# TensorE's instructions from the memory attention to the third head's state put into the program's own order, with dense matmuls dealt out behind each small step

## The chip, the cores and the metric

One core of one Trainium2 chip. The metric is device time in microseconds (us) of one launch. The kernel before was timed three times: median 1388.3 us, from 1385.67 to 1389.44.

## The reference, cut to what matters

One layer of a hybrid decoder, 1024 tokens of width 1024, all in fp32. One input projection feeds four HGRN2 heads (a gated recurrence), a sparse attention whose indexer picks 256 keys per query, and an attention into 256 memory tokens. Their outputs go through one output projection, and a SwiGLU feed-forward follows.

```python
h = rmsnorm(x, norm_mix[layer])
hq, hf, hi, hg, sq, sk, sv, iq, ik, iw, mq = split_in(h @ w_in[layer])
o_hg = hgrn2_mix(...)      # 4 heads; per chunk: o = q exp(b) S + (decayed q k^T) v; S = exp(b_last) S + k^T v
o_sa = dsa_mix(...)        # score, _, idx = lax.top_k(score, topk); softmax over the kept keys
o_mem = mem_mix(...)       # softmax(q k^T) v over 256 memory tokens
mixed = jnp.concatenate([o_hg, o_sa, o_mem], axis=-1)
x = x + (mixed @ w_out[layer]).astype(x.dtype)
a, b = jnp.split(rmsnorm(x, norm_ffn[layer]) @ w_ffn_in[layer], 2, axis=-1)
x = x + ((jax.nn.silu(a) * b) @ w_ffn_out[layer]).astype(x.dtype)
```

## The kernel before, in words

Every fp32 operand of a large product is split into a high and a low part, and the product is made of three passes (high by high, high by low, low by high). A projection of 128 output channels (`proj`, L165-190) is 24 matmuls of 128x512 for each half of the tokens, 48 in all; they are the dense work of the middle of the kernel. A page of weights comes by DMA through a staging tile (`load_page`, L117-L118): ScalarE (ACT) writes the high part, GpSimd (POOL) or VectorE (DVE) the low part. PSUM is used as four pairs of banks: `mm` for projections, `lg`, `sm` and `rc` for small products.

The stretch that the change touches goes from about 149 us (the indexer's scores are done) to 561 us (the sparse attention's softmax begins). It holds, in the order of the program's text:

- `hgrn_v(0)`: values of heads 0 and 1, token-major (`token_major`, L457: 192 matmuls of 128x256 into two `lg` and two `sm` banks, then eight scaled copies on ACT, L466).
- `memory_attention` (L689-724): 16 units, for 8 blocks of 128 tokens by 2 pairs of heads. A unit is logits (L697), maximum on DVE (L701), two Exp on ACT (L704), reciprocal (L706), scaling on POOL (L708), four transposes (L713), a copy (L715 on ACT or L717 on DVE), values (L722), a copy out (L724).
- for each head `hgrn_proj` (three projections of 48 matmuls, taken out of PSUM on DVE, L485), `hgrn_gates` (ACT and POOL), `hgrn_intra` (eight levels: a small product, L518 or L553, then `descend`: Q on DVE L527, K on POOL L528, F on DVE L529, and a masked copy L543), `hgrn_state` (transposes L571, L578, output products L594/L596, the square sums and norm on DVE L602/L144-151/L606, transposes L612, L613).
- sparse values (`token_major(4)`), sparse queries (pages 20 and 21), sparse keys (`sparse_keys`, pages 18 and 19, normed on DVE: L739, L144-151, L169, L172, L744), later split into the stacked keys `kst` (L811) and queries `qst` (L254).
- `bisect`, the top-k: 31 rounds over the bits of a threshold; a round counts scores, on DVE for blocks 7 and 4 (L646), on ACT as Sign for blocks 6, 5, 3 and 2 (L643), with a few tiny DVE operations (L638, L648, L655, L658) between the rounds.

No engine runs in the text's order. The kernel is built under a scheduler that simulates the engines (L1362: `schedule_with_timeline_sim=True`) and lays down one instruction list per engine; on the chip each engine runs its list strictly in order. So dense matmuls stand between small steps where the scheduler put them, and the bisection's counts fill DVE and ACT beside them.

All weight pages are issued from SP's queue. What the names in the rows are: `mat_` memory attention, `hg_` HGRN2, `sap_` projections and norms of the sparse attention, `sat_` the sparse attention itself, `idx_` indexer and top-k; `_mm`, `_lg`, `_sm`, `_rc` are the PSUM pairs, `whi`/`wlo` weights, `xn_h` the normed input.

Of the kernel before, what the change touches and what calls it, by code (L numbers as in the profile page):

```python
# [42 lines left out]
def hybrid_block(ctx, tc, xT, memT, wch, wikw, wv, wkm, wvm, woa, wob, wfi, wfo,  # L43
                 vec, cst, lvl, out):
    nc = tc.nc
    V, S, G, T = nc.vector, nc.scalar, nc.gpsimd, nc.tensor
# [400 lines left out]
    def token_major(g0):  # L447

        acc = [bank("lg"), bank("lg"), bank("sm"), bank("sm")]
        for g in range(2):  # L450
            w = load_page(wv[g0 + g], 4, 256)
            for tt in range(8):
                o = acc[tt // 2][:, 256 * (tt % 2):256 * (tt % 2) + 256]
                i = 0
                for pw, p in PASSES:
                    for k in range(4):
                        T.matmul(o, H[p][4 * g + k][tt // 4][:, bs(tt % 4)], w(pw, k),  # L457
                                 start=g == 0 and i == 0 and tt % 2 == 0,
                                 stop=g == 1 and i == 11 and tt % 2 == 1)
                        i += 1  # L460
        return [a.rearrange("p (t d) -> p t d", t=2) for a in acc]

    def scaled_rows(dst, acc):

        for tt in range(8):
            S.activation(dst[tt // 4][:, tt % 4, :], acc[tt // 2][:, tt % 2, :], AF.Copy,  # L466
                         scale=rn[:, tt:tt + 1])

    def hgrn_v(pair):
        ph[0] = "hg"  # L470
        Vp = [xt(10 + j, [128, 4, 256]) if pair else mt(4 + j, (128, 4, 256)) for j in range(2)]
        scaled_rows(Vp, token_major(2 * pair))
        for j in range(2):
            Vh[2 * pair + j] = lambda c, j=j: Vp[c // 4][:, c % 4, bs(j)]

    def hgrn_proj(h):
        ph[0] = "hg"
# [5 lines left out]
        for i, t in enumerate((Q, F, Gt)):  # L483
            proj(page(6 + 3 * h + i), 128, H,
                 lambda ps, hf: V.tensor_mul(t[:, hs(hf)], ps, rrow[:, hs(hf)]))  # L485
# [202 lines left out]
    def memory_attention():  # L688
        ph[0] = "mat"  # L689
        Pm, PTm = mt(2, (128, 2, 2, 256)), mt(3, (128, 2, 2, 2, 128))  # L690
        for b in range(8):
            for m in range(2):
                P, PT = Pm[:, m], PTm[:, m]
                lg = bank("lg").rearrange("p (j k) -> p j k", j=2)
                for j in range(2):
                    for p in range(2):
                        T.matmul(lg[:, j, :], mqs[2 * m + j][:, b // 4, bs(b % 4)],  # L697
                                 kms[m][:, j, p, :], start=p == 0, stop=p == 1)
                mx = np_.tile([128, 2], F32, tag="mx", name=nm("mx"))
                sm = np_.tile([128, 2], F32, tag="sm", name=nm("sm"))  # L700
                V.tensor_reduce(mx, lg, axis=AX.X, op=ALU.max)  # L701
                V.scalar_tensor_tensor(mx, mx, -1.0, qrs[:, m, b, :], op0=ALU.mult, op1=ALU.mult)
                for j in range(2):
                    S.activation(P[:, j, :], lg[:, j, :], AF.Exp, bias=mx[:, j:j + 1],  # L704
                                 scale=qrs[:, m, b, j:j + 1], accum_out=sm[:, j:j + 1])
                V.reciprocal(sm, sm)  # L706
                for j in range(2):
                    G.tensor_scalar(P[:, j, :], P[:, j, :], sm[:, j:j + 1], 1.0, op0=ALU.mult,  # L708
                                    op1=ALU.mult)
                tb = bank("rc").rearrange("p (j k q) -> p j k q", j=2, k=2)  # L710
                for j in range(2):
# [12 lines left out]
                S.activation(M[6 + m][:, bs(b)], po[:, 0:128], AF.Copy)  # L724
# [3 lines left out]
    def sparse_keys():  # L728
        ph[0] = "sap"
        kr.extend((mt(4), mt(5)))  # L730
        for m in range(2):
            def evac_k(ps, hf, m=m):
# [3 lines left out]
                S.activation(sq, ps, AF.Square)  # L736
                ss = bank("sm")
# [16 lines left out]
    def sparse_queries():  # L754
# [3 lines left out]
        def evac_q0(ps, hf):  # L758
            sums_q(qsq[:, 0], ps, hf)
            S.activation(sqr[0][:, hs(hf)], ps, AF.Copy)  # L760
# [605 lines left out]
```

## Time and profile before

| what | value |
|---|---|
| median of three runs | 1388.3 us |
| lowest, highest run | 1385.67, 1389.44 us |
| the profiled execution | 1389.85 us |
| its span | 1388.1 us |
| mean granted TensorE clock | 0.969 |
| busy share of the span, PE / DVE / ACT / POOL | 94% / 77% / 50% / 34% |

The span is the profiled time from the first instruction to the last; 1.75 us of the execution lie outside it. Busy shares are averages over stages with different limits: the busy time by stretch says more. Matmul durations overlap, so the cost of one matmul is read from the distance between starts.

### The profile page before, as it was taken

The numbers are of one execution on the slowest core, as the hardware profiler recorded it, in microseconds if no ns is written. First come the engines' busy times: TensorE is split into PE (matmuls) and PEld (weight loads), VectorE is DVE, ScalarE is ACT, GpSimd is POOL, SyncE is SP. The second block draws the span as 40 slices with busy tenths as digits, with TensorE's granted clock in tenths as the row PEclk, the third lists the DMA queues.
The fourth block names the chain that finished last, engine by engine and source line by source line (L and its number), as shares of the span: only waits on it lengthen the run. The fifth ranks groups of instructions, "written<-read, shape, count | busy, mean of one in ns | idle before, by whom it ended". The sixth has DMA issues, their size and how long they took to land.

```text
span 1388.1 us, 22034 instructions
## 1 busy us (share of the span) xinstructions
PE 1304.1 (94%) x8072; PEld 1067.2 (77%) x8072; DVE 1062.2 (77%) x2094; ACT 692.6 (50%) x1369; POOL 473.9 (34%) x395
## 2 busy tenths in 40 slices
PE   6989999988989995999997999999999998999998
PEld 4767787768878884776886888888888886878887
DVE  8697998896469689775579777777787766696764
ACT  7555879856853243657354333333333333334442
POOL 2311033355257632424005233332332310474520
PEclk9999999989999995899999999999999999999999
DMA  6210010000010001013331332223223219654241
GB/s 236 68 39 16 32 47 16 32 32 32 31 48 31 26 26 47 2 61 112 129 117 61 114 108 106 91 91 107 99 103 105 89 59 354 233 192 142 84 145 61
DMA packets 53244, 122.19 MB, mean 88 GB/s; under 512 B 6032, under 2 KB 6160, under 8 KB 53136
## 3 DMA queue, kind: packets, MB, share of 16 engines
q1 hardware_dynamic: 52848, 120.58, 25.4%
q8 instruction: 63, 1.03, 0.3%
q14 instruction: 45, 0.37, 0.1%
q10 hardware_dynamic: 288, 0.22, 0.1%
HBM read 92.19 MB, written 28.57 MB: 87 GB/s over the span
## 4 chain that ended last, share of the span: by engine, by line
PE 59%; DVE 6%; ACT 2%; issue 1%; POOL 1%; DMA 1%; ACTq 0%; DVEq 0%; POOLq 0%
PE ff_lg L1095 17%; PE ff_rc L1095 12%; PE fo_mm L1258 4%; PE fo_sm L1258 4%; PE wo_mm L1054 3%; PE fo_rc L1258 3%; PE fo_lg L1258 3%; PE wo_sm L1054 2%; PE sap_mm L186 2%; PE hg_mm L186 2%; PE sat_sm L856 1%; PE sat_lg L830 1%; PE wo_mm L186 1%; PE sat_rc L875 1%; PE sat_mm L875 1%
## 5 line engine op out<-in xcount | busy, mean ns | idle before, releaser
L117 ACT ACTIVATE ff_whi<-ff_x 128x512 fp32r<-128x512 f32 x112 | 70.0, 629 | 125.1 <-PE ff_rc L1095 69.1
L643 ACT ACTIVATE idx_x<-idx_x,packs 128x896 int8<-128x896 f32 (+3 forms) x128 | 105.7, 826 | 42.9 <-DVE packs L638 37.0
L1095 PE MATMUL ff_lg<-wo_h,ff_whi 128*128 128x512 f32 x396 | 104.3, 390 | 0.0
L186 PE MATMUL hg_mm<-xn_h,hg_whi 128*128 128x512 f32 x384 | 97.0, 396 | 0.0
L1095 PE MATMUL ff_rc<-wo_h,ff_whi 128*128 128x512 f32 x308 | 90.8, 395 | 0.0
L1095 PE MATMUL ff_lg<-wo_x,ff_whi 128*128 128x512 f32 x308 | 83.8, 400 | 5.3 <-ACT ff_tmp L1102 4.8
L118 DVE TENSOR_TENSOR ff_wlo<-ff_x,ff_whi 128x512 fp32r<-128x512 f32 x112 | 82.6, 746 | 6.9 <-ACT ff_whi L117 4.0
L1095 PEld LDWEIGHTS ff_lg<-wo_h,ff_whi 128*128 128x128 f32 x396 | 74.5, 188 | 15.5
L186 PEld LDWEIGHTS hg_mm<-xn_h,hg_whi 128*128 128x128 f32 x384 | 70.7, 188 | 14.5 <-issue 0.7
L118 POOL TENSOR_TENSOR hg_wlo<-hg_wst,hg_whi 128x512 fp32r<-128x512 f32 x32 | 42.9, 1353 | 104.9 <-ACT hg_whi L117 79.8
L1095 PEld LDWEIGHTS ff_lg<-wo_x,ff_whi 128*128 128x128 f32 x308 | 56.8, 189 | 23.8 <-ACT ff_whi L117 7.4
L646 DVE TENSOR_SCALAR_CACHE_REDUCE idx_x<-idx_x,packs 128x1024 int8<-128x1024 f32 x64 | 68.8, 1074 | 0.9
L1095 PEld LDWEIGHTS ff_rc<-wo_h,ff_whi 128*128 128x128 f32 x308 | 58.8, 191 | 12.5
L1095 PE MATMUL ff_rc<-wo_x,ff_whi 128*128 128x512 f32 x220 | 64.4, 390 | 0.1
L528 POOL TENSOR_TENSOR hg_x<-hg_x,hg_x 128x256 f32<-128x256 f32 x56 | 48.5, 881 | 30.4 <-PE hg_rc L518 18.8
L1095 PE MATMUL ff_lg<-wo_h,ff_wlo 128*128 128x512 f32 x198 | 55.6, 389 | 0.0
L388 DVE SCALAR_TENSOR_TENSOR idx_x<-idx_tmp,packs,idx_x 128x512 f32<-128x512 f32 (+2 forms) x70 | 46.1, 712 | 10.6 <-ACT idx_tmp L383 10.3
L118 DVE TENSOR_TENSOR fo_wlo<-fo_tmp,fo_whi 128x512 fp32r<-128x512 f32 x33 | 33.2, 1007 | 27.0 <-ACT fo_whi L117 27.0
L186 PE MATMUL hg_mm<-xn_h,hg_wlo 128*128 128x512 f32 x192 | 50.8, 397 | 0.0
L1095 PEld LDWEIGHTS ff_rc<-wo_x,ff_whi 128*128 128x128 f32 x220 | 41.2, 188 | 9.1 <-ACT ff_whi L117 0.6
L118 DVE TENSOR_TENSOR fo_wlo<-fo_h,fo_whi 128x512 fp32r<-128x512 f32 x31 | 32.0, 1033 | 19.0 <-ACT fo_whi L117 19.0
L1095 PE MATMUL ff_rc<-wo_h,ff_wlo 128*128 128x512 f32 x154 | 45.6, 389 | 0.0
(484 smaller groups left out, 3679.0 us busy)
## 6 DMA issues: line engine op xcount, KB each, us to landing
gd<-ff_m SPq DMA_DIRECT2D x77, 256.0 KB, 2.0
fo_x<-gd SPq DMA_DIRECT2D x77, 256.0 KB, 4.0
ff_x<-wfi SPq DMA_DIRECT2D x16, 512.0 KB, 3.3
ff_wst<-wfi SPq DMA_DIRECT2D x14, 512.0 KB, 3.3
ff_m<-wfi SPq DMA_DIRECT2D x14, 512.0 KB, 3.3
hg_wst<-wch SPq DMA_DIRECT2D x12, 512.0 KB, 3.3
fo_x<-wfo SPq DMA_DIRECT2D x24, 256.0 KB, 5.2
fo_h<-wfo SPq DMA_DIRECT2D x20, 256.0 KB, 4.2
```

Source lines behind the costliest of these rows:

```text
L117: S.activation(hi, src, AF.Copy)
L118: (eng or V).tensor_sub(lo, src, hi.bitcast(F32))
L186: T.matmul(ps[:M, :], w(pw, k), h[p][k][hf], start=i == 0, stop=i == len(order) - 1)
L388: V.scalar_tensor_tensor(sc[b][:, c0:c1], rl[:, :c1 - c0], iww[:, b, h:h + 1], sc[b][:, c0:c1], op0=ALU.mult, op1=ALU.add)
L528: G.tensor_mul(Kv[:, :, 0, :], Kv[:, :, 0, :], fr.to_broadcast([128, n, w]))
L643: S.activation(waste[S][:, :nk], sc[b], AF.Sign, bias=nf[:, j:j + 1], accum_out=ct[:, j:j + 1])
L646: eng.tensor_scalar(waste[eng][:, :nk], sc[b], fl[:, j:j + 1], None, op0=ALU.is_ge, op1=ALU.add, accum_out=ct[:, j:j + 1])
L830: T.matmul(lg[:, :c1 - c0], qst[h][b // 4][:, bs(b % 4)], kst[h][p][c][:, :c1 - c0], start=p == 0, stop=p == 1)
L875: T.matmul(po[ROWS[j], 0:128], sv[kb // 4][:, kb % 4, 128 * m + 64 * j:128 * m + 64 * j + 64], PTs[j][:, kb, :], start=kb == 0, stop=kb == ...
L1054: mm = T.matmul(ps, lhs, rhs, start=i == 0, stop=i == len(steps) - 1)
L1095: mm = T.matmul(ps, w[pw][:, bs(k)], HB[u][k][p], start=first and i == 0, stop=i == 11, skip_group_check=True)
L1258: T.matmul(banks[m], w[i][pw][:, bs(m)], b[i][p], start=first and i == 0 and n == 0, stop=i == NP - 1 and n == 2, skip_group_check=True)
```

## The change

Three things change, all of them between the end of the indexer's scores and the start of the sparse attention.

**Order.** A wrapper `InOrder` stands for TensorE. While it is on (from the memory attention to `hgrn_state(2)`), each TensorE instruction is to be issued after the one before it in the text. A generator `dense` yields one 128x512 matmul at a time, and `weave` puts n of them behind each small step: a head start of 48, then 10 behind each step of the memory attention, 24 behind each level of head 0, 21 behind the steps of head 0's state and of head 1, 20 behind those of head 2. The followers of a small reduction (`post`, `pend`) are put one step later. The memory attention's parts are taken apart into a pipeline: step s issues the transposes of unit s-2, the logits of unit s and the values of unit s-3.

**Values.** The three value projections (heads 0 and 1, heads 2 and 3, sparse) are made channel-major: 96 matmuls of 128x512 in the `mm` banks in place of 192 of 128x256 in `lg` and `sm`; DVE multiplies by the row scale, 16 transposes turn the result, ACT copies it out in four copies of 128x512.

**Place.** Queries (page 20) come with head 1's projections and both key pages (18, 19) before head 3's, where the keys came after head 3's gates. The text of the top-k's first part comes after head 3's gates as before, with `hgrn_state(2)` now ahead of it. `hgrn_intra(3)`, `hgrn_state(3)`, page 21, the sparse attention and all that follows keep their text.

```diff
+    class InOrder:
+        on, last = False, None
+        def go(self, f, *args, **kw):
...
+                with tc.issue_after(self.last):
+                    r = f(*args, **kw)
+            self.last = r.ins
...
-    def token_major(g0):
-
-        acc = [bank("lg"), bank("lg"), bank("sm"), bank("sm")]
...
-                        T.matmul(o, H[p][4 * g + k][tt // 4][:, bs(tt % 4)], w(pw, k),
...
+    def dense(tasks):
+
+        w = tasks[0][0]()
+        for n, (_, chains) in enumerate(tasks):
+            after = tasks[n + 1][0]() if n + 1 < len(tasks) else None
+            for steps, evac in chains(w):
+                ps = bank("mm")
+                for i, (lhs, rhs) in enumerate(steps):
+                    T.matmul(ps, lhs, rhs, start=i == 0, stop=i == len(steps) - 1)
+                    if i == len(steps) - 1:
+                        g = evac(ps)
+                        if g is not None:
+                            next(g)
+                            pend.append(g)
+                    yield
+            w = after
...
+        def turn(ps, j, hf):
+            t = tmp()
+            V.tensor_mul(t, ps, rrow[:, hs(hf)])
+            yield
+            tb = bank("sm")
+            for c in range(4):
+                T.transpose(tb[:, bs(c)], t[:, bs(c)], ident)
+            S.activation(dst()[hf][:, :, bs(j)], tb.rearrange("p (a b) -> p a b", a=4), AF.Copy)
...
+    def weave(steps, gen, n):
+
+        for _ in steps:
+            post()
+            take(gen, n)
...
+        units = [(b, m) for b in range(8) for m in range(2)]
+        for s in range(len(units) + 3):
+            ph[0] = "mat"
+            for d, stage in ((2, turn), (0, logits), (3, values)):
+                if 0 <= s - d < len(units):
+                    stage(*units[s - d])
+            yield
...
-    hgrn_v(0)
-    memory_attention()
-    hgrn_proj(0)
+    T.on = True
+    d = dense([hgrn_v_task(0)] + hgrn_tasks(0))
+    take(d, 48)
+    weave(memory_attention(), d, 10)
+    rest_of(d)
     hgrn_gates(0)
-    run(hgrn_intra(0))
-    hgrn_proj(1)
+    d = dense(hgrn_tasks(1) + [queries_task()])
+    weave(hgrn_intra(0), d, 24)
+    rest_of(d)
     hgrn_gates(1)
-    sparse_queries()
-    run(hgrn_state(0))
-    sparse_values()
-    hgrn_proj(2)
-    run(hgrn_intra(1))
-    hgrn_v(1)
-    run(hgrn_state(1))
+
+    def behind():
+        yield from dense([hgrn_v_task(1), sparse_values_task()])
+        yield from dense(hgrn_tasks(2))
+
+    d = behind()
+    weave(hgrn_state(0), d, 21)
+    weave(hgrn_intra(1), d, 21)
+    weave(hgrn_state(1), d, 21)
+    rest_of(d)
     hgrn_gates(2)
-    run(hgrn_intra(2))
-    hgrn_proj(3)
+    d = dense(keys_tasks() + hgrn_tasks(3))
+    weave(hgrn_intra(2), d, 20)
+    weave(hgrn_state(2), d, 20)
+    rest_of(d)
+    post()
+    post()
     hgrn_gates(3)
-    sparse_keys()
+    assert not pend
+    T.on = False
     bisect((7, 4), V, "v")
-    run(hgrn_state(2))
     bisect((6, 5, 3, 2), S, "s")
```

How the instruction lists move at three places. In the changed kernel every TensorE row carries the wrapper's line (L54 with the order off, L56 or L59 with it on), so rows are told by their tiles.

First, TensorE just behind the indexer's scores (`idx_rc`). Before, the value projection of heads 0 and 1 (L457) follows at once, with the square sums of the memory queries (`mat_sm`, L403) inside it:

```order
497 L380 MATMUL idx_rc_1426<-idx_x_52_192,idx_x_289_1243 128x512
498 L457 MATMUL hg_lg_1641<-hg_whi_1647,xn_h_127 128x256
499 L457 MATMUL hg_lg_1641<-hg_whi_1647,xn_h_131 128x256
500 L457 MATMUL hg_lg_1641<-hg_whi_1651,xn_h_135 128x256
501 L457 MATMUL hg_lg_1641<-hg_whi_1651,xn_h_139 128x256
502 L457 MATMUL hg_lg_1641<-hg_whi_1647,xn_h_128 128x256
```

The changed kernel at the same place:

```order
497 L54 MATMUL idx_rc_1426<-idx_x_52_192,idx_x_289_1243 128x512
498 L54 MATMUL mat_sm_1479<-packs,mat_tmp_1477 128x2 x4
499 L54 MATMUL mat_sm_1516<-packs,mat_tmp_1514 128x2 x4
500 L54 MATMUL mat_mm_1536<-xn_h_127,mat_whi_1528 128x512
501 L54 MATMUL mat_mm_1536<-xn_h_131,mat_whi_1528 128x512
```

The square sums and then the second page of memory queries (`mat_mm`) stand first; the value matmuls (`hg_mm`) begin at row 549.

Second, TensorE within the memory attention. Before, steps of two units stand close together, with single dense rows between:

```order
984 L697 MATMUL mat_lg_2231<-mkv_x_113_582,mat_x_337_1438 128x256 x2
985 L697 MATMUL mat_lg_2231<-mkv_x_113_582,mat_x_338_1439 128x256 x2
986 L697 MATMUL mat_lg_2257<-mkv_x_114_583,mat_x_339_1440 128x256 x2
987 L713 MATMUL mat_rc_2193<-packs,mat_m_382_1865 128x128 x2
988 L697 MATMUL mat_lg_2257<-mkv_x_114_583,mat_x_340_1441 128x256 x2
989 L186 MATMUL hg_mm_2815<-xn_h_176,hg_whi_2785 128x512
990 L713 MATMUL mat_rc_2193<-packs,mat_m_382_1865 128x128 x2
991 L186 MATMUL hg_mm_2815<-xn_h_180,hg_whi_2785 128x512
```

The changed kernel, one whole step with the last and first rows of the dense runs around it:

```order
750 L59 MATMUL mat_mm_2111<-xn_h_148,mat_whi_1909 128x512
751 L59 MATMUL mat_rc_2152<-packs,hg_m_389_1727 128x128 x4
752 L59 MATMUL mat_lg_2158<-mkv_x_114_583,mat_x_339_1440 128x256 x2
753 L59 MATMUL mat_lg_2158<-mkv_x_114_583,mat_x_340_1441 128x256 x2
754 L59 MATMUL mat_sm_2172<-hg_m_390_1728,mkv_x_115_584 64x128 x4
755 L59 MATMUL mat_mm_2111<-xn_h_152,mat_whi_1909 128x512
```

Each step is now transposes, logits and values of three different units, and exactly 10 dense rows lie between two steps.

Third, VectorE near the end of the last dense projection (page 21). Before, head 2's norm and state end (`hg_ro`, L606, L613) stands among the sparse attention's first masked exponents (`sat_x`, L832) and the queries' norm (`sap_abx`):

```order
980 L411 TENSOR_TENSOR packs<-packs 128x16
981 L151 SCALAR_TENSOR_TENSOR hg_ro_5137<-hg_abx_5159 128x8
982 L832 ISA sat_x_764_5706,sat_mz_5707<-sat_lg_5712,idx_x_154_807 128x512
983 L832 ISA sat_mz_5707 128x1
984 L144 TENSOR_SCALAR sap_abx_5638<-packs 128x32
985 L606 TENSOR_TENSOR hg_x_713_5135<-hg_rc_5138,hg_ro_5137 128x512
986 L606 TENSOR_TENSOR hg_x_713_5135<-hg_rc_5139,hg_ro_5137 128x512
```

The changed kernel:

```order
944 L174 SCALAR_TENSOR_TENSOR hg_ro_4683<-hg_abx_4727 128x8
945 L681 TENSOR_TENSOR hg_x_735_4681<-hg_rc_4684,hg_ro_4683 128x512
946 L681 TENSOR_TENSOR hg_x_735_4681<-hg_rc_4685,hg_ro_4683 128x512
947 L141 TENSOR_TENSOR wo_wlo_6330<-wo_wst_6327,wo_whi_6329 128x384
948 L558 TENSOR_TENSOR hg_m_659_3960<-hg_mm_4718,rrow 128x512
949 L141 TENSOR_TENSOR wo_wlo_6334<-wo_wst_6327,wo_whi_6333 128x256
950 L688 SCALAR_TENSOR_TENSOR hg_m_615_3614<-hg_rc_4766,packs,hg_m_615_3614 128x512
951 L688 SCALAR_TENSOR_TENSOR hg_m_615_3614<-hg_rc_4772,packs,hg_m_615_3614 128x512
952 L921 TENSOR_TENSOR sap_h_5364<-hg_m_673_4082,sap_h_5363 64x512
```

Head 2's norm and state end now stand whole before the first stacked key (`sap_h`, L921, the L811 of before), and the keys' own norm stands far ahead of them.

## Rows read from the trace of the kernel before

**Rows 1.** The page, part 1, TensorE: busy us, share, instructions.

```profile
PE 1304.1 (94%) x8072; PEld 1067.2 (77%) x8072; DVE 1062.2 (77%) x2094; ACT 692.6 (50%) x1369; POOL 473.9 (34%) x395
```

**Rows 2.** Busy by stretch: length, PE, PEld, DVE, ACT, POOL, PEclk, DMA share, GB/s.

```profile
149.00:187.00 38.00, 37.80 (x274) 35.70 (x273) 36.79 (x112) 30.10 (x62) 5.12 (x4) 1.00 0.09 29
187.00:278.50 91.50, 85.83 (x500) 67.20 (x499) 82.07 (x236) 81.33 (x197) 35.08 (x51) 0.98 0.09 30
278.50:342.00 63.50, 52.64 (x687) 45.62 (x687) 53.47 (x125) 38.42 (x84) 37.98 (x33) 0.89 0.10 34
300.00:320.00 20.00, 16.84 (x207) 15.02 (x208) 19.39 (x42) 14.24 (x30) 14.24 (x8) 0.74 0.00 1
342.00:390.00 48.00, 47.94 (x331) 41.93 (x332) 23.89 (x69) 38.54 (x86) 11.86 (x11) 1.00 0.10 34
390.00:430.00 40.00, 33.16 (x560) 30.59 (x559) 31.88 (x70) 19.62 (x45) 28.12 (x24) 0.96 0.09 28
430.00:520.00 90.00, 89.50 (x877) 75.02 (x875) 70.04 (x170) 29.97 (x53) 45.67 (x44) 1.00 0.11 32
520.00:561.00 41.00, 22.36 (x448) 17.88 (x448) 39.33 (x117) 15.60 (x26) 14.49 (x16) 0.57 0.11 40
561.00:1388.00 827.00, 806.27 (x3792) 654.12 (x3792) 604.97 (x940) 345.37 (x633) 261.62 (x182) 0.98 0.34 116
```

**Rows 3.** Waits of TensorE, 149 to 520 us: total us, times, longest.

```profile
PE hg_rc L518 <- DVE hg_x L527: 6.0, 6, 3.4
```

**Rows 4.** Groups by line, TensorE, 149 to 562 us: busy us, mean ns, idle before.

```profile
L186 PE MATMUL hg_mm<-xn_h,hg_whi 128*128 128x512 f32 x384 | 97.0, 396 | 0.0
L457 PE MATMUL hg_lg<-hg_whi,xn_h 128*128 128x256 f32 x128 | 19.4, 295 | 0.0
```

**Rows 5.** Timeline of TensorE at the value projection: start, duration, line, tiles, count.

```profile
148.98 1.11 PE L457 MATMUL hg_lg<-hg_whi,xn_h 128*128 128x256 f32 x8
149.93 0.64 PE L457 MATMUL hg_lg<-hg_wlo,xn_h 128*128 128x256 f32 x4
...
156.51 1.32 PE L186 MATMUL mat_mm<-xn_h,mat_whi 128*128 128x512 f32 x5
```

**Rows 6.** Timeline of TensorE in the memory attention: pairs of starts.

```profile
186.94 1.12 PE L697 MATMUL mat_lg<-mkv_x,mat_x 128*128 128x256 f32 x8
187.90 0.40 PE L186 MATMUL hg_mm<-xn_h,hg_whi 128*128 128x512 f32 x1
...
243.53 1.10 PE L722 MATMUL mat_sm<-mat_m,mkv_x 128*64 128x128 f32 x16
244.55 0.50 PE L186 MATMUL hg_mm<-xn_h,hg_whi 128*128 128x512 f32 x1
...
258.33 3.81 PE L186 MATMUL hg_mm<-xn_h,hg_whi 128*128 128x512 f32 x16
261.98 0.39 PE L186 MATMUL hg_mm<-xn_h,hg_wlo 128*128 128x512 f32 x1
```

**Rows 7.** Groups by line, DVE and ACT, 187 to 278.5 us.

```profile
L646 DVE TENSOR_SCALAR_CACHE_REDUCE idx_x<-idx_x,packs 128x1024 int8<-128x1024 f32 x19 | 24.2, 1276 | 0.4
...
L643 ACT ACTIVATE idx_x<-idx_x,packs 128x896 int8<-128x896 f32 x9 | 9.3, 1039 | 9.2 <-DVE packs L638 9.2
```

**Rows 8.** Timeline of TensorE: two levels of head 2.

```profile
462.89 0.76 PE L518 MATMUL hg_rc<-hg_x,hg_x 128*32 128x32 f32 x64
468.33 0.76 PE L518 MATMUL hg_rc<-hg_x,hg_x 128*32 128x32 f32 x64
```

**Rows 9.** Timeline of TensorE: the last dense matmuls and the first softmax transposes.

```profile
517.96 1.98 PE L186 MATMUL sap_mm<-xn_h,sap_wlo 128*128 128x512 f32 x8
...
561.12 1.11 PE L856 MATMUL sat_sm<-packs,sat_x 128*128 128x128 f32 x4 [0.93 <-POOL sat_x L847]
```

**Rows 10.** Waits of TensorE, 520 to 562 us: total us, times, longest.

```profile
PE sap_sm L172 <- DVE sap_tmp L169: 8.6, 1, 8.6
```

**Rows 11.** Groups by line, DVE, 508 to 561 us: the stacked keys.

```profile
L811 DVE TENSOR_TENSOR sap_h<-sap_m,sap_h 64x512 fp32r<-64x512 f32 x8 | 7.4, 927 | 1.1 <-PE sap_mm L186 0.9
```

More of the change, by code (lines that the diff above doesn't have):

```diff
@@ L463, in scaled_rows @@
[L463 to L477, printed above, removed]
+    pend = []
@@ new lines, in post @@
+    def post():
+        for g in pend[:]:
+            if next(g, pend) is pend:
+                pend.remove(g)
+    def dense(tasks):
[13 more added lines that the diff above has]
+            w = after
@@ new lines, in take, with rest_of, hgrn_v_task, dst @@
+    def take(gen, n):
+        for _ in range(n):
+            if next(gen, gen) is gen:
+                return False
+        return True
+    def weave(steps, gen, n):
+        for _ in steps:
+            post()
+            take(gen, n)
+    def rest_of(gen):
+        while take(gen, 24):
+            post()
+        post()
+    Vp = {}
+    def hgrn_v_task(pair):
+        def dst():
+            if pair not in Vp:
+                Vp[pair] = [xt(10 + j, [128, 4, 256]) if pair else mt(4 + j, (128, 4, 256))
+                            for j in range(2)]
+                for j in range(2):
+                    Vh[2 * pair + j] = lambda c, j=j: Vp[pair][c // 4][:, c % 4, bs(j)]
+            return Vp[pair]
+        return values_task(2 * pair, dst)
@@ new lines, in turn, with values @@
+        def turn(b, m):
+            P, PT = Pm[:, m], PTm[:, m]
+            tb = bank("rc").rearrange("p (j k q) -> p j k q", j=2, k=2)
+            for j in range(2):
+                for kb in range(2):
+                    T.transpose(tb[:, j, kb, :], P[:, j, bs(kb)], ident)
+            if m == 0:
+                S.activation(PT, tb, AF.Copy)
+            else:
+                V.tensor_copy(PT, tb)
+        def values(b, m):
+            PT = PTm[:, m]
+            po = bank("sm")
+            for kb in range(2):
+                for j in range(2):
+                    h = 2 * m + j
+                    T.matmul(po[ROWS[j], 0:128], vm[:, kb, 64 * h:64 * h + 64], PT[:, j, kb, :],
+                             start=kb == 0, stop=kb == 1, skip_group_check=True)
+            S.activation(M[6 + m][:, bs(b)], po[:, 0:128], AF.Copy)
@@ L744, in evac_k @@
                 V.scalar_tensor_tensor(o, o, vs[:, V_SAK:V_SAK + 1], r, op0=ALU.mult, op1=ALU.mult)
[L745 removed]
+            return normed
+        return [proj_task(18 + m, evac(m)) for m in range(2)]
     sv, sqr = [], []
[L749 to L762 removed]
```

140 lines of the change are left out of this document (78 added, 62 removed).

## The prediction

> **What bounds the kernel now.** I read the page's busy times first. TensorE is busy 1304.1 of 1388.1 us [rows 1], so what the change can gain is TensorE's idle time and its time at the lower clock. The busy times by stretch say where these lie [rows 2]. From 561 us to the end nothing is touched. The change works between 149 and 561 us: 371 us up to the end of the last dense matmuls near 520 [rows 9], and 41 us of tail.
>
> In the first part TensorE idles 0.2 + 5.7 + 10.9 + 0.1 + 6.8 + 0.5 = 24 us (length less busy, six stretches of [rows 2]; 300:320 lies inside one of them). The granted clock is below 1 in three stretches: 0.98, 0.89 and 0.96. The share below full speed, times the busy time, gives 1.7 + 5.8 + 1.3 = 9 us lost at 1.2 GHz. Together 33 us, so the true work at 2.4 GHz is 371 - 33 = 338 us. The waits name their cause: levels of the heads that stand for DVE's Q and F, the longest 3.4 us [rows 3].
>
> In the tail TensorE does 22.4 us of 41 at a clock of 0.57 while DVE is busy 39.3 [rows 2]; one wait of 8.6 us is for the keys' norm on DVE [rows 10]. There DVE sets the end. In the memory attention (187 to 278.5) three engines are near full at once: TensorE 85.8, DVE 82.1, ACT 81.3 of 91.5 [rows 2]. That stretch decides whether the change pays.
>
> **The change, part by part.**
>
> *Values.* Before, 8 matmuls of 128x256 take 149.93 - 148.98 = 0.95 us, 0.119 each [rows 5]; 192 cost 22.8 us. After, 96 of 128x512 at (261.98 - 258.33) / 16 = 0.228 [rows 6] cost 21.9, and 16 transposes come on top. (The means, 295 and 396 ns [rows 4], overlap and are no price.) The nearest small matmuls pace at 0.064 (values, 16 in 1.02 us) and 0.12 (logits, 8 in 0.96) [rows 6], so 1.0 to 1.9 us; I take 1.5. Three projections: 3 x (21.9 + 1.5 - 22.8) = **+2 us**. On DVE four products come to each, on ACT eight copies become four; neither engine bounds the places where these go. The weight loads are as many as before on SP's queue; nothing waits for them in [rows 3], so they cost nothing as long as the two weight pages of one value projection are split before the former one ends.
>
> *The hole at 149 us.* Before, the value matmuls run from 148.98 while both `mm` banks are being emptied; the memory queries go on at 156.51 [rows 5]. After, the values stand behind those queries and themselves need `mm`. What is left for TensorE is two square sums. Bounds: 0 if the banks come free at once, 7.5 if nothing runs. The banks wait for ACT and DVE, both busy before as after, so I take **+6**.
>
> *The head start.* From 156.5 the list holds 46 query matmuls, the 48 of the head start and the square sums: 94 x 0.228 + 2 = 23 us, to 180. Before, the first logits come at 186.94 [rows 6], and what they need (the queries' norm on DVE) is not moved forward. Bounds 0 and 7; some transposes of the values fit in: **+5**.
>
> *The memory attention.* TensorE's rows are now 202 dense (19 steps of 10, and 12) and 16 units. A unit is 0.48 logits, 0.51 values [rows 6] and four transposes between the two paces above, 1.3 to 1.5 in all. 202 x 0.228 + 16 x 1.4 = 68 us. DVE and ACT have no less to do than before: the list of DVE holds the same 38 counts (19 at 1.28 us [rows 7] and 19 shorter) and the same 16 maxima, and sums to 82 us at the durations of before; ACT's to 77. So the stretch can't end before 82 us, and at before's DVE share, 82.1 / 91.5 = 0.90, it takes 91. I take 86, nearer to the lower end, since part of that lost tenth was DVE and ACT waiting for TensorE's products. TensorE idles 86 - 68 = **+18** (14 to 23).
>
> *The clock there.* TensorE would be busy 79% of this stretch. The two nearest rows are 390:430 (83% busy, clock 0.96) and 300:320 (84%, 0.74) [rows 2]. At 0.96 the work fits into the idle time; at 0.74 it takes 68 / 0.74 = 92 us, 6 more than I allow. I take **+3** for this and the hole, between 0 and 6. The Trainium skill (Perfetto Trace Analysis, Matmul Optimizations) says that TensorE's power follows its use, so matmuls should be issued back to back in batches; that speaks against cutting the dense work into runs of 10. By it the sum would carry +6 or more here; 187:278.5, cut up no less and at 0.98 [rows 2], speaks for the smaller price.
>
> *Levels and states.* Some 36 small steps, each behind 20 to 24 dense matmuls, some 5 us of cover. In 342:390 and 430:520 the list of before already has about that, a level every 468.33 - 462.89 = 5.4 us [rows 8], and TensorE idles 0.6 us in 138 [rows 2]. So the step's chain (product, DVE's Q, POOL's K) fits, and the holes of 278.5:342 and 390:430 should close. I take **+4** for all steps and the joints of the projections; if a third of them wait 1 us it is 12, if none 0. What is queued behind a waiting step is now all the dense work, as nothing may pass it.
>
> *The tail.* Keys and their norms move in front of head 3's projections, head 2's norm and state end in front of the first stacked key. On DVE's new list the rows from the first stacked key (0.93 us for one [rows 11]) to the first softmax's input sum to 33 us at before's durations. They can start once head 2's state is out, 40 dense matmuls, 9 us, before the end. So the tail is 24 us at least; I take 29, with 5 of waits, against 561.1 - 520 = 41 [rows 9]: **-12** (-17 to 0, the latter if page 21 must be awaited first).
>
> *Sum.* Waits and clock: 6 + 5 + 18 + 3 + 4 = 36 for the 33 of before, so +3; work +2; tail -12: **-7 us**. The dense work would end at 525 rather than 520, and the softmax start at 554 rather than 561. Against the profiled execution, 1389.85, that is 1383; this execution is 1.55 above the median of the three runs, so 1381. With each term at its end the forecast's own range is 1370 to 1391.
>
> **Rivals.**
>
> *The wait moves into the memory attention* (slower). TensorE may not pass a step, and each step needs probabilities two steps old, from DVE, ACT and POOL, whose lists are filled with bisection counts that wait for each other: ACT stands 9.2 us there for the next threshold [rows 7]. If the two lists don't pack better than before and TensorE's lateness comes on top, the stretch takes 81.3 + 9.2 + 9 = 100 us, idle is 32 rather than 18, and the clock costs 4 more: 1381 + 18 = 1399. The change turns to a loss where the stretch passes 93 us. For it: DVE at 90% before. Against: each part has two steps, over 7 us, to be ready.
>
> *All holes close* (faster). If DVE's and ACT's counts slide behind the units, the stretch is TensorE's own, 72 us; hole and levels fall to 3 and 0, the tail to 24: 14 + 3 + 4 + 5 = 26 less, 1355, or some of it, up to 1367. Against: lists are strict, and the counts stand between the units' rows.
>
> *It does little.* Before's lists already have dense runs behind most levels (342:390, 430:520 [rows 2]); if the tail, too, waits for page 21, the time is 1388 to 1392.
>
> *The clock falls for the whole stretch.* With runs of 10 between waits TensorE would stay mostly at 1.2 GHz, as in 520:561 (0.57 [rows 2]): 68 / 0.57 = 119 us, +33, 1414. That is what the rule of the skill named above would give at its worst; 187:278.5 speaks against it.
>
> **How the numbers follow.** Forecast 0.42, moved wait 0.22, holes close 0.20, little 0.10, clock 0.06. A measurement of this kernel can tell 0.3%, 4.2 us, from no change. The forecast lies two thirds below 1384.1, a quarter within, the rest above 1392.5. Faster: 0.29 + 0.20 = 0.49. Same: 0.10 + 0.10 = 0.20. Slower: 0.03 + 0.22 + 0.06 = 0.31. The range, 1362 to 1400, takes in the forecast and the near ends of the rivals and leaves out most of the closing holes and the clock's fall. As cases of both signs hold most of the chance, the forecast's own range, 1370 to 1391, stands beside it.
>
> **What would show it.** Right: TensorE idle near 6 us just behind 149; a memory attention of 82 to 91 us with DVE near full and TensorE under 80% busy; levels with next to no wait at a clock of 1; the last dense matmul near 525 and the first softmax transposes near 554. Wrong: a memory attention over 93 us, waits of a microsecond at many levels, or a tail still near 41 us.

## The result, and the profile after

The changed kernel takes 1425.8 us (median of 4 runs, 1424.62 to 1426.74) against 1387.19 us before (4 runs): a ratio of 1.029, 95% interval 1.0267 to 1.0314. It was forecast at 1381, range 1362 to 1400. It is 38.6 us slower, and the profiled execution shows where. TensorE by stretch (columns as in [rows 2]):

```profile
149.00:187.00 38.00, 33.05 (x148) 27.50 (x149) 36.78 (x112) 28.98 (x59) 2.56 (x2) 0.89 0.05 15
187.00:280.00 93.00, 79.04 (x440) 60.53 (x439) 78.40 (x247) 78.86 (x190) 29.35 (x45) 0.90 0.07 23
280.00:520.00 240.00, 212.99 (x2199) 174.80 (x2198) 168.69 (x417) 112.52 (x234) 114.60 (x104) 0.94 0.10 32
149.00:560.00 411.00, 364.44 (x2996) 295.96 (x2996) 306.02 (x819) 238.09 (x512) 161.84 (x165) 0.93 0.09 28
```

The dense work ends at 560 instead of 520. In those 411 us TensorE idles 46.6 us (length less busy), and 7% below full speed on 364 us of busy time is another 25: 72 us lost, against 33 before, worked out in the same way from [rows 2]. The work itself, 339 us, is what it was.

TensorE's waits over the whole part (total us, times, longest), the changed kernel:

```profile
PE hg_rc L59 <- POOL hg_x L603: 15.7, 7, 6.7
PE mat_rc L59 <- POOL hg_m L783: 13.9, 4, 4.9
PE hg_rc L54 <- DVE hg_x L611: 8.6, 2, 8.0
PE hg_rc L54 <- DVE hg_x L602: 5.1, 6, 1.7
PE hg_sm L59 <- DVE hg_tmp L507: 4.8, 3, 2.6
PE hg_sm L59 <- ACT hg_tmp L854: 3.4, 1, 3.4
```

The rows with L59 are those issued in the text's order. The largest two are levels that wait for K from GpSimd (L603, the L528 of before) and transposes of the memory attention that wait for probabilities (L783, the L708 of before). Before, the levels' longest waits were for VectorE's Q [rows 3], and waits for K came to 5.5 us: two rows of the waits before, from 149 to 562 us, and 0.4 in the transposes behind the levels (one L59 row of the changed kernel holds all three places).

```profile
PE hg_rc L518 <- POOL hg_x L528: 3.0, 3, 2.5
PE hg_rc L553 <- POOL hg_x L528: 2.1, 2, 1.4
```

The last three kinds of row are new or moved: the turn of the channel-major values (L507), the queries' square sums (L854), and head 3's levels in the tail (L611, L602).

The longest wait in the levels costs twice. TensorE's timeline around it:

```profile
320.15 0.65 PE L59 MATMUL hg_rc<-hg_x,hg_x 128*32 128x32 f32 x32 [6.72 <-POOL hg_x L603]
321.35 0.66 PE L59 MATMUL hg_rc<-hg_x,hg_x 128*32 128x32 f32 x32 [0.55 <-POOL hg_x L603]
321.94 5.56 PE L59 MATMUL hg_mm<-xn_h,hg_whi 128*128 128x512 f32 x16
327.33 1.98 PE L59 MATMUL hg_mm<-xn_h,hg_wlo 128*128 128x512 f32 x8
329.15 3.79 PE L59 MATMUL hg_mm<-xn_h,hg_whi 128*128 128x512 f32 x16
332.77 1.97 PE L59 MATMUL hg_mm<-xn_h,hg_wlo 128*128 128x512 f32 x8
```

After 7.3 us of waiting, 16 dense matmuls take 327.33 - 321.94 = 5.39 us, at a granted clock of 0.67; the next 16 of that kind take 332.77 - 329.15 = 3.62, at 1.00. So the restart costs 1.8 us more. The rule weighed in the prediction (the Trainium skill, Perfetto Trace Analysis, Matmul Optimizations: back to back in batches) has the trace on its side in direction: as TensorE's busy share of the memory attention's stretch went from 94% to 85%, its clock went from 0.98 to 0.90.

What GpSimd does during that wait (its timeline):

```profile
305.63 1.60 POOL L603 TENSOR_TENSOR hg_x<-hg_x,hg_x 128x256 f32<-128x256 f32 x2
307.22 2.67 POOL L576 TENSOR_SCALAR hg_x<-hg_x,packs 128x512 f32<-128x512 f32 x1
309.87 1.81 POOL L577 TENSOR_SCALAR hg_x<-hg_x,packs 128x512 f32<-128x512 f32 x1
311.66 2.85 POOL L755 TENSOR_SCALAR idx_x<-idx_x,packs 128x640 int8<-128x640 f32 x1
314.48 2.68 POOL L141 TENSOR_TENSOR hg_wlo<-hg_wst,hg_whi 128x512 fp32r<-128x512 f32 x2
317.25 2.10 POOL L761 TENSOR_SCALAR idx_x<-idx_x 128x1024 f32<-128x1024 f32 x1
319.43 1.87 POOL L603 TENSOR_TENSOR hg_x<-hg_x,hg_x 128x256 f32<-128x256 f32 x2
```

Between the K of one level and the K of the next GpSimd works without a gap for 12 us: gates of the next head (L576, L577), two operations of the top-k's masks (L755, L761) and two weight splits (L141). The cover of a level is 24 dense matmuls, 24 x 0.228 = 5.5 us at the pace of [rows 6].

The tail goes from the last dense matmuls, which end at 560.3, to the softmax transposes:

```profile
558.37 1.97 PE L54 MATMUL sap_mm<-xn_h,sap_wlo 128*128 128x512 f32 x8
...
598.12 1.97 PE L54 MATMUL sat_sm<-packs,sat_x 128*128 128x128 f32 x8
```

That is 37.8 us, against 561.1 - 519.9 = 41.2 before [rows 9].

### The profile page after: what moved, and what is told of

Read it like the earlier page. It is cut to its first block, busy times and chain, and to the rows that moved or that the text cites. A ratio compares the mean times of both kernels' runs of the same rounds, so it can differ in the third digit from the quotient of the medians.

```text
span 1424.9 us, 21563 instructions
## 1 busy us (share of the span) xinstructions
PE 1319.5 (93%) x7832; PEld 1063.6 (75%) x7832; DVE 1064.3 (75%) x2106; ACT 692.8 (49%) x1357; POOL 472.3 (33%) x395
## 4 chain that ended last, share of the span: by engine, by line
PE 61%; DVE 8%; ACT 2%; issue 1%; POOL 1%; DMA 1%; ACTq 0%; DVEq 0%; POOLq 0%; SPq 0%
PE ff_lg L54 17%; PE ff_rc L54 12%; PE hg_mm L59 6%; PE wo_mm L54 4%; PE fo_mm L54 4%; PE fo_sm L54 4%; PE fo_lg L54 3%; PE fo_rc L54 3%; PE wo_sm L54 2%; PE hg_rc L59 2%; PE sat_sm L54 1%; ACT idx_x L718 1%; PE sat_lg L54 1%; PE sat_mm L54 1%; PE sat_rc L54 1%
## 5 line engine op out<-in xcount | busy, mean ns | idle before, releaser
L59 PE MATMUL hg_mm<-xn_h,hg_whi 128*128 128x512 f32 x543 | 140.5, 408 | 0.5 <-ACT hg_whi L140 0.5
L59 PEld LDWEIGHTS hg_mm<-xn_h,hg_whi 128*128 128x128 f32 x543 | 104.6, 197 | 23.0 <-ACT hg_whi L140 1.2
L54 PE MATMUL ff_lg<-wo_h,ff_whi 128*128 128x512 f32 x396 | 104.4, 390 | 0.0
L141 POOL TENSOR_TENSOR hg_wlo<-hg_wst,hg_whi 128x512 fp32r<-128x512 f32 x38 | 50.6, 1352 | 121.8 <-ACT hg_whi L140 43.5
L54 PE MATMUL ff_rc<-wo_h,ff_whi 128*128 128x512 f32 x308 | 90.8, 395 | 0.0
L54 PE MATMUL ff_lg<-wo_x,ff_whi 128*128 128x512 f32 x308 | 84.0, 401 | 5.3 <-ACT ff_tmp L1212 4.8
L141 DVE TENSOR_TENSOR ff_wlo<-ff_x,ff_whi 128x512 fp32r<-128x512 f32 x112 | 82.6, 746 | 6.5 <-ACT ff_whi L140 4.0
L54 PEld LDWEIGHTS ff_lg<-wo_h,ff_whi 128*128 128x128 f32 x396 | 74.5, 188 | 15.5
L54 PEld LDWEIGHTS ff_lg<-wo_x,ff_whi 128*128 128x128 f32 x308 | 57.0, 190 | 24.0 <-ACT ff_whi L140 7.4
L59 PE MATMUL hg_mm<-xn_h,hg_wlo 128*128 128x512 f32 x272 | 69.6, 393 | 0.0
L54 PEld LDWEIGHTS ff_rc<-wo_h,ff_whi 128*128 128x128 f32 x308 | 58.8, 191 | 12.4
L54 PE MATMUL ff_rc<-wo_x,ff_whi 128*128 128x512 f32 x220 | 64.4, 390 | 0.1
L603 POOL TENSOR_TENSOR hg_x<-hg_x,hg_x 128x256 f32<-128x256 f32 x56 | 46.3, 842 | 48.7 <-PE hg_rc L59 23.0
L59 PEld LDWEIGHTS hg_mm<-xn_h,hg_wlo 128*128 128x128 f32 x272 | 50.7, 189 | 10.4
L54 PE MATMUL ff_lg<-wo_h,ff_wlo 128*128 128x512 f32 x198 | 55.6, 389 | 0.0
L141 DVE TENSOR_TENSOR fo_wlo<-fo_tmp,fo_whi 128x512 fp32r<-128x512 f32 x33 | 33.2, 1007 | 27.0 <-ACT fo_whi L140 27.0
L54 PEld LDWEIGHTS ff_rc<-wo_x,ff_whi 128*128 128x128 f32 x220 | 41.2, 188 | 9.1 <-ACT ff_whi L140 0.5
L141 DVE TENSOR_TENSOR fo_wlo<-fo_h,fo_whi 128x512 fp32r<-128x512 f32 x31 | 32.8, 1059 | 17.6 <-ACT fo_whi L140 17.5
```

What stands on the lines that cost most here:

```text
L54: return f(*args, **kw)
L59: r = f(*args, **kw)
L141: (eng or V).tensor_sub(lo, src, hi.bitcast(F32))
L603: G.tensor_mul(Kv[:, :, 0, :], Kv[:, :, 0, :], fr.to_broadcast([128, n, w]))
```

## The experiments

Two theories to begin with. S: the strict order makes TensorE stand at small steps. V: the new values and the new places cost the time.

**x1_free, x2_mem_order, x3_lvl_order**: the order is taken off in whole or in part. In x1 the line goes that turns it on ahead of the values, in x2 one that turns it off is put ahead of `hgrn_gates(0)`, and in x3 it is turned on only there.

```diff
x1:
-    T.on = True
x2:
+    T.on = False
     hgrn_gates(0)
x3:
-    T.on = True
...
+    T.on = True
     hgrn_gates(0)
```

> The change with the wrapper never on: same text, same values, same places, but the scheduler may order TensorE's rows as it likes. Theory S (the strict order makes TensorE stand at small steps while dense work waits behind them): most of the 38 us goes, 1385 to 1397. Theory V (the new form of the values, with its transposes behind a DVE product, and the new places cost the time): it stays at 1415 or more.

> The change with the order on from the values to the end of the memory attention only. In the changed kernel the stretch up to the first level of head 0 lost 30 of the 70 us that TensorE lost (idle and lower clock), before it lost about 8. Theory S: about 10 us above the kernel without any order. Theory V: no difference from it.

> The change with the order on from head 0's gates to head 2's state only. Theory S: the levels lost 28 us of waits and 11 of clock, so 20 to 30 us above the kernel without any order. Theory V: no difference from it.

Measured: 1394.2 us without any order (1.0058, 1.0035 to 1.008 of before), 1404.1 with it in the memory attention, 1416.4 with it in the levels. So 10 us and 22 us (x3's four runs lie between 1408.5 and 1419.2), 32 together; the whole change is 31.6 above x1, and S holds. Stretches of x1, then of x2 and x3:

```profile
187.00:280.00 93.00, 86.63 (x598) 67.53 (x596) 83.50 (x244) 80.25 (x194) 36.79 (x51) 0.98 0.11 35
280.00:520.00 240.00, 223.02 (x2179) 182.31 (x2180) 172.05 (x447) 117.37 (x245) 116.36 (x108) 0.96 0.10 30
```

```profile
187.00:280.00 93.00, 78.76 (x461) 60.33 (x460) 79.61 (x250) 78.87 (x190) 29.15 (x45) 0.91 0.07 23
280.00:520.00 240.00, 227.69 (x2271) 185.44 (x2270) 168.20 (x427) 117.65 (x246) 124.21 (x112) 0.97 0.11 35
```

```profile
187.00:280.00 93.00, 80.63 (x546) 62.01 (x548) 83.03 (x251) 79.59 (x193) 32.92 (x48) 0.91 0.09 29
280.00:520.00 240.00, 214.42 (x2146) 176.31 (x2136) 170.94 (x428) 114.76 (x238) 113.53 (x103) 0.94 0.10 31
```

TensorE's busy time falls from 86.6 to 78.8 of 93 us, and its clock from 0.98 to 0.91, where the order is on in the memory attention; from 223 to 214 of 240, and from 0.96 to 0.94, where it is on in the levels. The times of the two parts add up, but their places don't. In x3 the order is off in the memory attention, and yet that stretch loses 93 - 80.63 x 0.91 = 19.6 us (idle and lower clock), against 93 - 86.63 x 0.98 = 8.1 in x1: about half of what x3 loses more than x1 up to 520 us. With the order on in the memory attention alone, the levels of x2 lose 19.1 us, less than the 25.9 of x1. The scheduler makes another list wherever it is still free, so 10 and 22 us are the prices of these two kernels, not of the strict order at two places, and that they sum to 32 is in part luck.

The rest, x1 against before, is 7 us.

**x4_values, x6_free_token, x10_places, x11_pipeline**: the parts of those 7 us, with the scheduler free. x4, x10 and x11 edit the kernel before, x6 edits x1: there `hgrn_v(0)`, `hgrn_v(1)` and `token_major(4)` stand as before in place of the three values tasks, the two later ones ahead of head 0's state, and the dense matmuls are dealt out 5 and 9 behind a step instead of 10 and 21. x11 takes the new `memory_attention`, its steps run one after the other.

```diff
x4:
-        scaled_rows(Vp, token_major(2 * pair))
+        channel_major(2 * pair, Vp)
x10:
-    hgrn_gates(1)
     sparse_queries()
+    hgrn_gates(1)
...
+    sparse_keys()
     hgrn_proj(3)
     hgrn_gates(3)
-    sparse_keys()
+    run(hgrn_state(2))
     bisect((7, 4), V, "v")
-    run(hgrn_state(2))
```

> The kernel before with the channel-major values alone, in the old places, order left to the scheduler. Theory S: within 5 us of the kernel before (2 us more TensorE work). Theory V: 10 us or more above it.

> The change without the order and with the token-major values of before, the two later value projections ahead of head 0's state. What is left of the change is the memory attention's pipeline and the new places of queries and keys. If the channel-major values cost what they cost alone (14 us) and the rest gives back what the free kernel suggests (7 less), it takes 1376 to 1384 and is the fastest here. If the values' cost is of the scheduler's making and not of their form, it takes 1388 to 1396.

> The kernel before with the new places alone: queries ahead of head 1's gates, keys ahead of head 3's projections, head 2's state ahead of the top-k's first part. The prediction put 12 us of gain on this (the tail from 41 to 29). If that holds: 1374 to 1382. If VectorE's work is the same wherever it stands: within 5 us of before.

> The kernel before with the memory attention's parts written as the three-step pipeline, nothing else, order left to the scheduler. If the text's order only matters through the strict order: within 5 us of before. If the scheduler's order follows it and gets worse: 5 to 15 above.

Measured: x4 1401.4 (1.0107), x6 1401.2 (1.0095), x10 1398.7 (1.0074), x11 1387.1 (1.0001, 0.9988 to 1.0014). The values alone cost 14 us, as V had it and S had not, yet x1 with the old values is slower, by 5 to 7 us. (x6 differs from x1 in where the values stand and how the dense work is dealt out, too.) x6 and x10 came out beyond every time that was expected of them. The parts don't add up, so with the scheduler free a price of one part can't be carried into another list. One thing does repeat: with channel-major values the hole at 149 us is there (x1 and x4, a wait of 2.7 us each), with token-major ones it isn't (x6, x10). The pipeline's text costs nothing by itself. The places, on which the forecast put its gain, cost 11 us. Yet the tail of x10 is shorter:

```profile
530.33 1.98 PE L186 MATMUL sap_mm<-xn_h,sap_wlo 128*128 128x512 f32 x8
...
563.75 1.09 PE L856 MATMUL sat_sm<-packs,sat_x 128*128 128x128 f32 x8 [0.53 <-POOL sat_x L847]
```

It takes 563.75 - 532.3 = 31.4 us in place of 41.2. But the dense work ends at 532.3 instead of 519.9, and from the softmax's start to the end of the span x10 needs 1399.0 - 563.75 = 835.3 us where the kernel before needed 1388.1 - 561.1 = 827.0.

**x5_masks_dve, x12_no_masks**: what makes the levels late. x5 moves both operations of the masks to VectorE; x12 returns from `bisect` ahead of the loop that makes the masks, so that loop (counts, scan and masks) is missing from its time and the softmax reads scores that are not masked.

```diff
x5:
-            G.tensor_scalar(eq, sc[b], fl[:, j:j + 1], None, op0=ALU.is_equal)
+            V.tensor_scalar(eq, sc[b], fl[:, j:j + 1], None, op0=ALU.is_equal)
...
x12:
-        for j, b in enumerate(blocks):
-            nk = 128 * (b + 1)
-            gt, eq = waste[V][:, :nk], waste[G][:, :nk]
...
+        return
```

> The change with the two GpSimd operations of each top-k mask (equality and the last scaling, twelve rows of 0.5 to 3 us) on VectorE. Theory Q1 (levels are late because GpSimd's strict list puts mask work in front of a level's K): the waits for GpSimd's K fall from 15.7 to under 6 us and the time by 8 to 15, to 1411 to 1418. Theory Q2 (the levels are late whoever does the mask work, since VectorE's list is as full there): the waits move to VectorE's Q and F, and the time stays within 5 us of 1425.8.

> The changed kernel with all 31 rounds of counts but without the mask work behind them (comparison, scan and the two GpSimd operations for each of six blocks are left out, so the sparse attention reads raw scores). Theory M (mask work in front of K on GpSimd and of Q and F on VectorE makes the levels late): the waits of levels and states for K, Q and F between 280 and 520 us, 16 in the changed kernel, fall under 4. Theory C (the counts do): they stay over 10. Removing the work itself could save little more, as TensorE has 240 us to do there.

Measured: x5 1422.0, x12 1412.7. Waits of x5:

```profile
PE hg_rc L59 <- DVE hg_x L602: 8.4, 3, 3.2
...
PE hg_rc L59 <- POOL hg_x L603: 2.5, 4, 1.1
```

Waits of x12 from 280 to 520 us:

```profile
PE hg_sm L59 <- ACT hg_tmp L843: 6.8, 1, 6.8
PE hg_sm L59 <- DVE hg_tmp L507: 2.9, 2, 2.7
PE hg_sm L59 <- DVE hg_rk L184: 2.5, 1, 2.5
PE hg_rc L59 <- DVE packs L849: 1.7, 1, 1.7
PE hg_rc L59 <- POOL hg_x L603: 1.1, 2, 0.5
```

With the mask work on VectorE the waits for K fall from 15.7 to 2.5 and 8.4 us of waits for Q and F appear: both theories were half right, and some 4 us are gained (x5's four runs lie between 1414.4 and 1424.1). Without the mask work, on either engine, the waits for K are 1.1 us, no wait for Q or F is left, and the kernel is 13 us faster. So M holds for these waits: the masks make the levels late. GpSimd is only the first place where they stand in the way. It is not the whole loss of the stretch, which in x12 is

```profile
280.00:520.00 240.00, 223.87 (x2266) 184.20 (x2267) 139.56 (x395) 117.89 (x245) 90.05 (x97) 0.95 0.10 33
```

TensorE still loses 240 - 223.87 x 0.95 = 27 us there, against 40 in the changed kernel; 13 of the 27 are waits of the projections' followers (the `hg_sm` rows), and the kernel is still 25 us above before. The kernel before and x1 were not run without the masks, so how much of the 13 us gained is the strict order waiting for them and how much is their own work stays open.

**x7_before_8, x8_after_8**: 8 bisection rounds in place of 31, in both kernels.

```diff
-        for bit in range(30, -1, -1):
+        for bit in range(30, 22, -1):
```

> The kernel before with 8 of the 31 bisection rounds; the other 23, and with them the right top-k, are left out. It is the partner of the next run. Some 23 x 2.2 us of counts go from VectorE and 23 x 3.7 from ScalarE between 155 and 410 us. Expected 5 to 15 us faster than with all rounds, since TensorE loses 33 us in all up to 520.

> The changed kernel with 8 of the 31 bisection rounds; the other 23 are left out. Theory C (the bisection's counts, which stand in VectorE's and ScalarE's lists between the steps, make the steps late, so that a strict order has to wait): the difference to its partner falls from 38 to under 20 us, and the waits for the memory attention's probabilities from 13.9 to under 4. Theory L (a step's own chain is too long for its cover): the difference stays over 30 and those waits over 10.

Measured: 1363.1 and 1398.3, 35.2 us apart instead of 38.6. The kernel before gains 25 us, where 5 to 15 were expected. Its masks now run before 280 us, its rounds end early, and TensorE has no hole left in the levels:

```profile
280.00:480.00 200.00, 199.84 (x2289) 173.69 (x2288) 102.87 (x229) 55.87 (x105) 91.91 (x95) 1.00 0.11 37
```

In x8 the levels are better, too: from 280 to 520 us TensorE loses 240 - 234.60 x 0.99 = 8 us, and the waits for K are 1.6 us in all, which agrees with x12. The memory attention is no better. Its waits for probabilities are 15.7 us, none less, although VectorE is now busy 62 and ScalarE 59 of the stretch's 93 us:

```profile
187.00:280.00 93.00, 77.27 (x423) 58.73 (x422) 61.98 (x142) 59.14 (x143) 57.32 (x57) 0.87 0.07 23
```

That does not clear the other engines. With so few rounds the masks move into this stretch: GpSimd is busy 57 us in it instead of 29, and its mask rows, at 189 to 206 and 232 to 262 us, stand among the scalings of the probabilities that the transposes wait for. One such place (L755 is a mask, L783 the scaling; the transposes behind it waited 3.4 us, to 253.95):

```profile
251.87 1.57 POOL L755 TENSOR_SCALAR idx_x<-idx_x,packs 128x512 int8<-128x512 f32 x1
253.41 1.83 POOL L783 TENSOR_SCALAR hg_m<-hg_m,mat_sm 128x256 f32<-128x256 f32 x2
```

So x8 shows that fewer counts don't help the memory attention as long as other work takes their place; it doesn't decide between theory C and theory L.

**x9_lag3, x13_late, x14_late_free**: more cover. x9 puts the transposes and the values of the memory attention one step later behind the logits, with four tiles for probabilities instead of two and a head start of 40 instead of 48; x13 is x9 with one more `yield` in each follower of a projection and the extra `post()` calls that go with it, x14 is x13 with the order never on.

```diff
+        Ps, PTm = [mt(2, (128, 2, 2, 256)), mt(1, (128, 2, 2, 256))], mt(3, (128, 2, 2, 2, 128))
...
+            for d, stage in ((3, turn), (0, logits), (4, values)):
...
-    take(d, 48)
+    take(d, 40)
```

> The change with one more step between a unit's logits and its transposes (four probability tiles instead of two, 20 steps, head start 40): the dense cover of the chain of maximum, two Exp, reciprocal and GpSimd's scaling grows from two steps to three, from some 7.4 to 11 us. Theory L (the chain, with table loads and gate work of the head on ScalarE between, is longer than two steps at some units): the waits for the probabilities fall from 13.9 to under 5 us and the time to 1408 to 1418. Rival (the stretch is bound by ScalarE's and VectorE's work): the waits move to other rows of it and the time stays within 5 us of 1425.8.

> The kernel of x9_lag3 with the followers of a projection (the turn of the values, the keys' square sums and norm rows, the queries' square sums) one step later. Theory L (each wait is a chain longer than its cover, and the waits add up): the waits of hg_sm rows, 12 us in the changed kernel, fall under 4 and the time to 1396 to 1404. Rival (waits only move to the next row, since VectorE and GpSimd are late by their lists anyway): the time stays within 4 us of 1409.3.

> The same text with the order never on. If the strict order is what costs, it is faster than x13_late and near x1_free (1394). If enough cover makes the strict order harmless, the two are within 4 us of each other.

Measured: x9 1409.3, x13 1404.4, x14 1389.0. The memory attention in x9, stretch and wait:

```profile
187.00:280.00 93.00, 86.51 (x614) 67.86 (x613) 80.91 (x254) 77.38 (x190) 36.04 (x50) 0.96 0.09 29
```

```profile
PE mat_rc L59 <- POOL hg_m L783: 3.3, 2, 2.1
```

One more step of lag takes the waits for probabilities from 13.9 to 3.3 us, TensorE's busy time from 79.0 to 86.5 and the clock from 0.90 to 0.96, and 16.5 us off the kernel. In x13 the waits of the followers fall from 11.7 us (four rows) to 2.0, but only 5 us come off: 12.8 us for K remain there, and 4.4 for a copy of the memory attention. Against x14 the strict order still costs 15 us. More cover at fixed distances helps each step that gets it; it doesn't reach the levels, where the lateness is 12 us at a time.

**x15_pipe3**: the kernel before with the memory attention of x9, order left to the scheduler (a diff as in x11).

> The kernel before with the memory attention written with the longer lag and four probability tiles, order left to the scheduler. The kernel before waits some 5 us there for probabilities. If the four tiles free the scheduler from those waits: 1378 to 1384, faster than both kernels. If not: within 5 us of before.

Measured: 1383.4 us, 0.9977 (0.9961 to 0.9993) of before. Of the kernels that leave nothing out it is the fastest, 4 us below before, at the near edge of what was expected.

## Why the prediction was wrong

**The bound** was read rightly: between 149 and 561 us the time is TensorE's work, its waits and its clock. What it waits for was read in part: the prediction named VectorE's Q and F, and the 5.5 us for GpSimd's K stand in the same view. The accounts close: 72 us lost instead of 33, some 1 us more work, a tail 3.4 us shorter, +37 in the profiled executions (1426.74 - 1389.85).

**Values, +2**: right as work. Their turns also wait (L507, 4.8 us, and 2.0 more at 184 us), which the step left out.

**The hole, +6, and the head start, +5**: 38.0 - 33.05 = 5.0 us idle to 187 us and 0.11 x 33 = 3.6 of clock, 8.6 for the 11 forecast. The first logits came at 181 instead of 187 us, so the second term was read wrongly: the logits do not need the queries' norm that I took them to wait for. The Exp behind them does, and the first probabilities then waited 4.1 us, in the next stretch.

**The memory attention, +18 and +3 of clock**: 14.0 us idle and 0.10 x 79 = 7.9 of clock, 22 in all. The size was right, the split and the reason were not. I had VectorE and ScalarE set the length by their work. x9 left that work and took the waits away. The chain of a unit is longer than two steps at four units, and the trace shows why: other work stands in a strict list ahead of it. The first wait (4.1 us) is the norm. In the second (2.7) GpSimd splits three weight tiles, 3.8 us, just ahead of the scaling. In the third (2.2) and the last (4.9) head 0's gates come in between. Here is the last, on GpSimd (L576 and L577 are gates):

```profile
266.02 0.69 POOL L576 TENSOR_SCALAR hg_x<-hg_x,packs 128x512 f32<-128x512 f32 x1 [6.85 <-ACT hg_x L574]
266.71 0.77 POOL L577 TENSOR_SCALAR hg_x<-hg_x,packs 128x512 f32<-128x512 f32 x1
267.45 0.94 POOL L783 TENSOR_SCALAR hg_m<-hg_m,mat_sm 128x256 f32<-128x256 f32 x2
```

VectorE's reciprocal for this scaling was done at 264.45; GpSimd stood 6.85 us for ScalarE's sigmoid first, which came behind two loads of activation tables of 1.28 us each (at 261.49 and 264.00). These four readings are of the trace; no run took one of these rows away.

**Levels and states, +4 (at most 12)**: this is the step that failed. From 280 to 560 us TensorE idles 46.6 - 5.0 - 14.0 = 27.6 us, and the clock takes some 14 more: 41 us in place of 4. The idle time is the 15.7 us of waits for K and 11.7 of waits for the followers of projections (the four `hg_sm` rows), which the step had not counted at all. Two things were wrong. The holes did not close: from 280 to 520 us x1, without any order, loses 26 us, and the kernel before loses 25 from 278.5 to 520 [rows 2]. And with the strict order 14 us came on top (40 in the changed kernel). I argued from 342:390 and 430:520 [rows 2], where dense runs of the same size hid a level. Those are the calm stretches: the rows of the masks take 20.3 us in 278.5:342 and 20.9 in 390:430, the stretches with idle time, none in 342:390 and 12.1 in 430:520. The sentence "the holes should close" had nothing to rest on: what else stood in GpSimd's and VectorE's lists there was in the trace and was not looked for. x12 shows for the changed kernel that the masks make K late, and in x7 the holes of the list of before are gone once masks and counts are out of that stretch; which of the two it was there, no run tells apart.

**The tail, -12**: -3.4. The stacked keys are written where the normed input lay, and that is read by the last dense matmuls, so a part of page 21 has to be awaited. ScalarE's and VectorE's first rows of them, the changed kernel:

```profile
551.50 5.21 ACT L920 ACTIVATE sap_h<-hg_m 64x512 fp32r<-64x512 f32 x8 [1.57 <-PE sap_mm L54]
```

```profile
554.33 2.40 DVE L921 TENSOR_TENSOR sap_h<-hg_m,sap_h 64x512 fp32r<-64x512 f32 x2 [2.09 <-PE sap_mm L54]
```

Both wait for matmuls of page 21. ScalarE starts 8.8 us before the dense work ends, close to the 9 of the forecast, VectorE only 6.0 us before. From there VectorE needs 43.8 us to the transposes, where its rows of before summed to 33 and 5 were allowed for waits. It is busy for 42.7 of the 43.8, so what was mis-sized is the rows' time and not the waiting. Of the 8.8 us that the tail is longer than the 29 forecast, 3 are the later start and 6 the longer run. In x10, with the places alone and the scheduler free, the tail did fall by 9.8 us, and the gain was lost at both ends of it: so a short tail was to be had, and it was not worth what I took it for.

**The range**: the sum of the terms at their ends is not the 1370 to 1391 given. The bounds as written (hole 0 to 7.5, head start 0 to 7, memory attention 14 to 23, clock 0 to 6, levels 0 to 12, values 0 to 3, tail -17 to 0) make some 1353 to 1414. The measured time lies beyond that, too, by the levels.

**The rivals**: "the wait moves into the memory attention" had the sign, the mechanism (TensorE may not pass a late step) and a price of 18 us; what moved there was no more than the forecast itself had. The waits came up in the levels. That rival should have been asked of every small step of the list, not of one stretch. "The clock falls for the whole stretch" was nearest in time (1414), but not in mechanism: the clock was 0.90 in the memory attention, and of the 72 us lost 25 are clock and 47 idle time.

## What to carry to other kernels

A strict order turned every late small step into idle time on the engine that is the bound, and the restart at a lower clock into more; ask of each step how long its chain takes with what else stands in the other engines' lists at that place, not in the calmest stretch. Cover must be as long as the worst chain: here one more step of lag was worth 16 us, while evenly dealt runs failed where other engines had 12 us of work in a row. At a wait, look at what stands in the releasing engine's list just ahead of the releaser. And before work is counted as moved forward, look for whose buffer it writes and what will run beside it.

## What the runs showed that was not expected

The same GpSimd operation takes very different times beside a busy VectorE: the gate scaling L576 took 2.67 us at 307 us, next to a scan on VectorE, and 0.70 at 247 us. So the 12 us that made the longest wait are not all amount of work: at the shortest times that rows of these lines and shapes take in this trace and in x8's they would be 0.69 + 0.76 + 1.89 + 2.52 + 1.05 = 6.9 us, an estimate. In the tail VectorE's key rows (L921) took 0.68 us at the fastest and 1.68 at the slowest, the slow ones while GpSimd ran the same kind of row for 13.56 us without a gap:

```profile
554.39 13.56 POOL L921 TENSOR_TENSOR sap_h<-hg_m,sap_h 64x512 fp32r<-64x512 f32 x8 [3.11 <-PE sap_mm L54]
```

That may be part of why 33 us of rows became 42.7; no run here took the two engines apart.

With the scheduler free, prices of parts did not add: +14 for the values, +11 for the places and 0 for the pipeline alone, and +7 for all of them together, with the dense work dealt out anew.
